# Moving the sample's attention from the attention units to the output projection in a one-core streaming encoder layer

## The chip, the cores and the metric

The kernel runs on one core of one Trainium2 chip. The metric is the device time of one execution in microseconds (us); the number given for a kernel is the median of its runs.

## What is computed

One layer of an encoder over two groups of tokens that share their weights: a prompt of 1,024 tokens and a sample of 64 tokens with a cache of 1,024 past tokens. The model width is 1,024, the feed-forward width 4,096, everything in float32. Shift, scale and gate come from a small product with `w_ada`.

```
h   = RMSNorm(x) * (1 + scale1) + shift1
u   = h @ w_in                -> diff q|k|v (4 heads of 128), sb q|k|v (8 heads of 64)
diff: p = softmax(q k^T / 8 - slope * dist, chunk mask), a = p0 - lam * p1, o = RMSNorm(a v) * 0.8
sb:   w[i,j] = sigmoid(z[i,j]) * product over later keys of sigmoid(-z), o = w v
x   = x + gate1 * RMSNorm(mix @ w_out)
x   = x + gate2 * RMSNorm(relu(h2 @ w_up)^2 @ w_down)
outputs: x of prompt and sample, and the new k and v of both groups
```

The prompt attends to itself. The sample attends to the cache and to itself, so each of its heads has 1,088 keys.

## The kernel before

Every product is done in split form: a float32 matrix is cast into a high part (ACT, L64) and a low part, the difference (DVE or POOL, L65), and two or three matmuls of these parts are summed in PSUM. The 1,088 tokens lie in nine tiles of 128, the ninth holding the sample's 64.

Attention is cut into eight units u of 128 columns: units 0 to 3 are one differential head each (class Diff), units 4 to 7 two stick-breaking heads each (class Stick). A unit's section is eight steps. A step has two parts: `score` (products of queries and keys, then softmax or sigmoids and a scan) and `apply` (transposes of the weights on PE, their split, product with the values). One loop runs through all steps and merges the apply of step j with the score of step j+1; beside them a filler hands out pieces of the projections of the next unit, so that PE has work while DVE and ACT prepare weights. Scans (L712) and the products after them (L713) are on DVE, sigmoids (L738, L739) and exponentials (L624) on ACT.

The sample is one more kind of step, class Sample, one per unit, put into the sections: sample u lies in the section of unit u+1, sample 3 at the end of its own section, sample 7 before the last step. Its score transposes the cache's keys (L813), splits them, and multiplies (L836 to L838); for units 4 to 7 it takes sigmoids (L867, L868), masks the corner on POOL (L720), and scans; its apply transposes (L586), multiplies with the values (L602, L603) and reduces; `finish` writes the result `ms` to `mixD` in DRAM (L908). Its split keys and values take four of the ten large buffers "qk" that also hold the units' Q and K.

After the last step comes the output projection. The weights w_out are split (POOL for the low part), `mixD` is read back and split for three groups of tiles, and for each of nine tiles PE does 48 matmuls (32 for the ninth) into two PSUM banks "pv" and "qk":

```
for m in range(NTT):
    ...
    ps = bank(f"py{m}{i}", "qk" if i else "pv")
    ...
    if pend:
        tail_T(*pend.pop())
```

After a tile's matmuls follows its epilogue: product with the gate (DVE, L1076), squares and sums (ACT, L87), an inverse root on POOL (L80, L81), the addition to x (DVE, L1079), squares again, again POOL, a scaling (ACT, L1083). One tile later `tail_T` transposes the result and makes h2 from it (L163, L276, L278, L64, L65). Then come sixteen blocks of the feed-forward part, up (L303 to L305) and down (L1145 to L1148).

The order of the instructions on each engine is fixed when the kernel is built: a scheduler takes the instructions by their place in the program and by its own estimate of when each can start, and an engine then works through its queue in the order that results. A buffer tag with n buffers lets the next tile of that tag begin when the oldest is released.

Of the kernel before, what the change touches and what calls it, by code (L numbers as in the profile page):

```python
# [10 lines left out]
F32 = mybir.dt.float32  # L11
# [23 lines left out]
def build(tc, I, O):  # L35
# [755 lines left out]
    class Sample:  # L791
# [6 lines left out]
        def cache(self):  # L798
            u = self.u
            fam, uc = family(u)  # L800
            kr = big(f"ckr{u}", "raw", [P, 8, P], F32)
            load(kr, ck[fam][:, :, uc : uc + P])
            vr = big(f"cvr{u}", "raw", [P, 8, P], F32)
            load(vr, cvv[fam][:, :, uc : uc + P])
            kn = small([P, 2, TS], f"kn{u}", "kf")
            load(kn, smD[u])
            vn = small([TS, P], f"vn{u}", "kf")
            load(vn, smV[u])
            kh, kl = (big(f"ck{x}{u}", "qk", [P, PAST]) for x in "hl")
            for half in range(2):  # L810
                ps = bank(f"pck{u}{half}", "qk")
                for i in range(4):
                    nc.tensor.transpose(ps[:, i * P : (i + 1) * P], kr[:, 4 * half + i, :], ident)  # L813
                cols = slice(512 * half, 512 * half + 512)
                split(ps, kh[:, cols], kl[:, cols])
# [6 lines left out]
            self.keys = [(kh[:, 0:512], kl[:, 0:512]), (kh[:, 512:], kl[:, 512:]), (Kn[:, 0, :], Kn[:, 1, :])]  # L822
            Vn = brief([TS, 2, P], f"Vn{u}", "Vn", F32R, bufs=1)
            split(vn, Vn[:, 0, :], Vn[:, 1, :])
            V = []
            for i in range(2):
                v = big(f"cv{u}{i}", "qk", [P, 4, 2, P])
                split(vr[:, 4 * i : 4 * i + 4], v[:, :, 0, :], v[:, :, 1, :], el=nc.gpsimd)
                V.append(v)
            self.V = lambda j: V[j // 4][:, j % 4] if j < 8 else Vn  # L830
# [45 lines left out]
        def apply(self):  # L876
            u, s = self.u, self.s
            po = bank(f"po{self.name}", "pv")
# [85 lines left out]
    for u in range(7):  # L964
        if u != 3:
            sections[u + 1].insert((1,1,2,2,1,1,2)[u], Sample(u))
    sections[3].append(Sample(3))
    sections[7].insert(8, Sample(7))
    steps = [st for sec in sections for st in sec]
    need = []  # L970
    for u in range(8):
        sec = [st for st in sections[u] if not isinstance(st, Sample)]
        for st, g in zip((sec[0], sec[2], sec[6]), range(3)):
            need.append((steps.index(st), (u, g)))
# [53 lines left out]
    for g, (c0, n) in enumerate(GRP):  # L1028
        hi, lo = mT[g]
        for k in range(KT):  # L1030
            st = big(f"mst{g}{k}", "s", [P, 512], F32)
            load(st[:, :n], mixD[k, :, c0 : c0 + n])
            split(st[:, :n], hi[:, k, :n], lo[:, k, :n])
            if g == 2:
                nc.vector.tensor_tensor(hi[:, k, 320:384], st[:, 256:320], fr(hi[:, k, 256:320]), ALU.subtract)
# [11 lines left out]
    for m in range(NTT):  # L1047
# [6 lines left out]
        for i in range(2):  # L1054
            ps = bank(f"py{m}{i}", "qk" if i else "pv")
            cols = slice(512 * i, 512 * i + 512)
            for k in range(KT):
# [14 lines left out]

# [11 lines left out]
        pend.append((m, xn))  # L1084

# [184 lines left out]
```

## Time and profile before

| | |
|---|---|
| median of 3 runs | 1585.93 us (1582.46 to 1588.23) |
| the profiled execution, its own time | 1589.58 us |
| its span in the profile | 1587.9 us |
| PE busy | 1517.0 us, 96% of the span |
| DVE busy | 987.2 us, 62% |
| ACT busy | 703.3 us, 44% |
| POOL busy | 366.7 us, 23% |

The profile is of one execution. PE is the matmul engine, DVE the vector engine, ACT the scalar engine, POOL the general engine, SP the one that issues DMAs. Busy time counts a matmul from its start to its modelled end, and matmuls overlap, so that 96% does not mean that PE has no room. PEclk is the granted clock of PE as a share of 2.4 GHz; its lower level is 1.2 GHz, and a value between is a mean over the stretch. The windows view gives for a stretch its length, then the busy time (and the number of instructions) of PE, of PEld (weight loads, which overlap PE), DVE, ACT and POOL, then PEclk, the share of DMA time and GB/s. In the timeline a row is start, length, engine, line, operation, out<-in and shape, with the idle time before it and who ended it in brackets. A line such as L712 is a line of the kernel before.

### The profile page before, as it was taken

To read this page: it belongs to the slowest core of one execution; us is meant where nothing else is said; L and a number is where in the kernel's file an instruction comes from. 1 tells how busy PE (TensorE), PEld (TensorE's weight loads), DVE (VectorE), ACT (ScalarE), POOL (GpSimd) and SP (SyncE) were. 2 spreads that over 40 slices of the span, in tenths; PEclk is the share of its full clock that TensorE was granted. 3 is DMA by queue.
4 is the path that set the end of the run, shared out by engine and by line. 5 is a ranking of instruction groups with operands and counts; after the bars stand their busy time and mean duration, and the time that the engine had idled before them with its cause. 6 is when DMAs were issued, how large, how long until landed. Compare 5 with 4: busy or idle time off the path is not lost.

```text
span 1587.9 us, 23684 instructions
## 1 busy us (share of the span) xinstructions
PE 1517.0 (96%) x8682; PEld 1357.9 (86%) x8682; DVE 987.2 (62%) x1880; ACT 703.3 (44%) x1665; POOL 366.7 (23%) x580
## 2 busy tenths in 40 slices
PE   6899999999999999789999999999999999999998
PEld 3689988988888889667889888999999899999896
DVE  3777676778789888995552455445544445544447
ACT  3867675766666667656563221121221121221132
POOL 0444352526353434451120000000000000000003
PEclk9999999998999999879999999999999999999999
DMA  9322142432322222364220222021111011111025
GB/s 309 115 60 87 55 116 84 135 95 76 95 74 85 69 70 78 103 208 161 97 63 27 80 80 78 17 79 53 54 42 52 28 41 53 54 41 53 27 80 179
DMA packets 152518, 133.22 MB, mean 84 GB/s; under 512 B 11233, under 2 KB 136274, under 8 KB 152402
## 3 DMA queue, kind: packets, MB, share of 16 engines
q1 hardware_dynamic: 152402, 131.71, 27.2%
q8 instruction: 68, 1.11, 0.3%
q14 instruction: 48, 0.39, 0.1%
HBM read 108.59 MB, written 23.09 MB: 83 GB/s over the span
## 4 chain that ended last, share of the span: by engine, by line
PE 74%; DVE 12%; issue 4%; ACT 3%; DMA 2%; POOL 1%; SPq 0%; POOLq 0%; DVEq 0%; ACTq 0%
PE pu L303 8%; PE pu L304 8%; PE pu L305 8%; PE pd L1145 8%; PE pd L1146 8%; PE pd L1148 7%; DVE k L712 4%; PE py L1059 2%; PE py L1060 2%; PE pt L586 2%; DVE s L713 2%; PE py L1062 2%; PE pq L304 1%; PE pq L303 1%; PE pq L305 1%
## 5 line engine op out<-in xcount | busy, mean ns | idle before, releaser
L1152 DVE TENSOR_TENSOR acc<-pd,acc 128x512 f32<-128x512 f32 x252 | 171.9, 687 | 113.3 <-PE pd L1148 107.2
L1130 ACT ACTIVATE sq<-pu 128x384 f32<-128x384 f32 (+1 forms) x96 | 45.2, 471 | 310.8 <-PE pu L305 310.8
L1131 DVE TENSOR_TENSOR sq<-sq 128x384 f32<-128x384 f32 (+1 forms) x96 | 72.1, 751 | 174.7 <-ACT sq L1130 174.7
L65 DVE TENSOR_TENSOR al<-pt,ah 128x512 fp32r<-128x512 f32 (+2 forms) x128 | 75.5, 599 | 25.7 <-ACT ah L64 24.9
L575 PE MATMUL pz<-K,Q 128*128 128x512 f32 (+2 forms) x192 | 74.8, 393 | 6.4 <-ACT k L739 2.2
L64 ACT CAST ah<-pt 128x512 fp32r<-128x512 f32 (+2 forms) x128 | 65.4, 523 | 33.6 <-PE pt L586 23.2
L586 PE MATMUL pt<-ident,s 128*128 128x128 f32 x432 | 73.7, 288 | 3.3 <-DVE s L713 2.6
L624 ACT ACTIVATE s<-s,mn 128x512 f32<-128x512 f32 (+3 forms) x96 | 58.5, 611 | 26.7 <-DVE mn L660 25.4
L576 PE MATMUL pz<-Kl,qz 128*128 128x512 f32 (+2 forms) x192 | 69.8, 369 | 0.0
L712 DVE TENSOR_TENSOR_SCAN k<-k 128x127 f32<-128x127 f32 (+3 forms) x64 | 62.1, 980 | 4.3 <-POOL k L720 4.0
L713 DVE TENSOR_TENSOR s<-s,k 128x383 f32<-128x383 f32 (+3 forms) x96 | 62.9, 662 | 1.4
L586 PEld LDWEIGHTS pt<-ident,s 128*128 128x128 f32 x432 | 53.1, 147 | 7.6 <-DVE s L713 3.3
L65 DVE TENSOR_TENSOR rl<-sq,rh 128x384 fp32r<-128x384 f32 x64 | 35.7, 558 | 37.9 <-ACT rh L64 37.9
L738 ACT ACTIVATE s<-pz 128x512 f32<-128x512 f32 (+2 forms) x96 | 48.1, 501 | 16.5 <-PE pz L576 12.0
L575 PEld LDWEIGHTS pz<-K,Q 128*128 128x128 f32 x192 | 38.3, 200 | 15.1 <-ACT k L739 4.5
L64 ACT CAST rh<-sq 128x384 fp32r<-128x384 f32 x64 | 32.9, 514 | 40.2 <-DVE sq L1131 38.2
L739 ACT ACTIVATE k<-pz 128x512 f32<-128x512 f32 (+2 forms) x96 | 48.4, 504 | 4.9 <-DVE k L712 4.0
L442 POOL CAST qz<-Q 64x256 fp32r<-64x256 f32 x64 | 34.7, 542 | 66.3 <-PE pz L576 63.9
L760 PE MATMUL po<-al,V 128*128 128x256 f32 (+1 forms) x160 | 43.5, 306 | 6.7 <-DVE al L65 6.6
L759 PE MATMUL po<-ah,V 128*128 128x256 f32 (+1 forms) x160 | 44.9, 292 | 0.5 <-ACT ah L64 0.5
L720 POOL TENSOR_SCALAR_AFFINE_SELECT s<-s 128x128 f32<-128x128 f32 x64 | 30.1, 470 | 63.6 <-ACT s L738 62.9
L660 DVE CUSTOM_DVE_ANT_0 s<-pz,T 128x512 f32<-128x512 f32 (+3 forms) x64 | 37.2, 585 | 10.8 <-PE pz L576 10.3
(1227 smaller groups left out, 5211.3 us busy)
## 6 DMA issues: line engine op xcount, KB each, us to landing
arr<-in_w_ada SPq DMA_DIRECT2D x16, 512.0 KB
arm<-in_w_ada SPq DMA_DIRECT2D x16, 512.0 KB
ar<-in_w_ada SPq DMA_DIRECT2D x10, 512.0 KB
mixD<-mx SPq DMA_DIRECT2D x32, 128.0 KB
xr<-in_x_prompt SPq DMA_DIRECT2D x16, 256.0 KB
xD<-xr SPq DMA_DIRECT2D x16, 256.0 KB
xy<-xD SPq DMA_DIRECT2D x8, 512.0 KB
out_y_prompt<-xy SPq DMA_DIRECT2D x16, 256.0 KB
```

The source lines that it names most:

```text
L64: (eh or nc.scalar.copy)(hi, src)
L65: (el or nc.vector).tensor_tensor(lo, src, fr(hi), ALU.subtract)
L303: mm(ps[:, :n], lhsT=wh[:, k, :], rhs=hh[:, k, :n], start=(k == 0), stop=False)
L304: mm(ps[:, :n], lhsT=wh[:, k, :], rhs=hl[:, k, :n], start=False, stop=False)
L305: mm(ps[:, :n], lhsT=wl[:, k, :], rhs=hh[:, k, :n], start=False, stop=(k == 7))
L575: mm(ps[:, :w], lhsT=S["Q"][m][:, qt], rhs=S["Kd"][m][:, c0 : c0 + w], start=True, stop=False)
L586: nc.tensor.transpose(pt[:kr, i * P : (i + 1) * P], a, ident)
L712: nc.vector.tensor_tensor_scan(k, k, k, 1.0 if c == n - 1 else kp[c + 1][:, 0:1], ALU.mult, ALU.bypass)
L1145: mm(ps, lhsT=rh[:, off : off + P], rhs=wh[:, cols], start=(j == 0), stop=False)
L1146: mm(ps, lhsT=rh[:, off : off + P], rhs=wl[:, cols], start=False, stop=(m == 8 and end))
L1148: mm(ps, lhsT=rl[:, off : off + P], rhs=wh[:, cols], start=False, stop=end)
L1152: nc.vector.tensor_tensor(acc[m][:, cols], ps, acc[m][:, cols], ALU.add)
```

## The change

The eight samples leave the sections. After the weights w_out and the prompt's part of `mixD` have been read, a new loop runs the samples' applies and scores, merged as the steps were, and the output projection's token tiles 0 to 7 become generators that the same filler hands out between them, each counted as 10.9 us, the samples as 6.3 us. The sample's columns of `mixD` are read and split after sample 7, and only then comes tile 8. The sample's split keys become four tiles of 512 columns with the tag "s" (11 buffers, shared with the sample's weights and tables, with x, xn and the pieces of `mixD`); its values become one tile with the tag "v" (2 buffers, of which the gate's rows hold one), split at the start of apply and not in score. A token tile's two PSUM banks come from "pj" (2 banks in all) and no longer from "pv" and "qk", of which the samples now use these.

```diff
-            kh, kl = (big(f"ck{x}{u}", "qk", [P, PAST]) for x in "hl")
+            self.keys = []
             for half in range(2):
...
+                kh, kl = (big(f"ck{x}{u}{half}", "s", [P, 512]) for x in "hl")
+                split(ps, kh, kl)
+                self.keys.append((kh, kl))
...
+        def values(self):
...
+            V = big(f"cv{u}", "v", [P, 8, 2, P])
             for i in range(2):
-                v = big(f"cv{u}{i}", "qk", [P, 4, 2, P])
-                split(vr[:, 4 * i : 4 * i + 4], v[:, :, 0, :], v[:, :, 1, :], el=nc.gpsimd)
+                js = slice(4 * i, 4 * i + 4)
+                split(self.vr[:, js], V[:, js, 0, :], V[:, js, 1, :], el=nc.gpsimd)
...
         def apply(self):
             u, s = self.u, self.s
+            self.values()
...
-    for u in range(7):
-        if u != 3:
-            sections[u + 1].insert((1,1,2,2,1,1,2)[u], Sample(u))
-    sections[3].append(Sample(3))
-    sections[7].insert(8, Sample(7))
...
-    for m in range(NTT):
+    def out_tile(m):
...
-            ps = bank(f"py{m}{i}", "qk" if i else "pv")
+            ps = bank(f"py{m}{i}", "pj")
...
+                yield 0.68
...
+    for m in range(8):
+        fill.add(out_tile(m), 10.9)
+    samples = [Sample(u) for u in range(8)]
+    drain(samples[0].score())
+    for j, st in enumerate(samples):
+        nxt = samples[j + 1] if j < 7 else None
+        ratio = fill.left() / sum(x.cost for x in samples[j:])
+        for c in merge(st.apply(), nxt.score() if nxt is not None else ()):
+            fill.spend(c * ratio)
+        if j:
+            samples[j - 1].finish()
+    samples[7].finish()
+    for x in fill.todo:
+        drain(x[0])
+    fill.todo = []
+    mixed(2, TP, TS, 256, "s")
+    drain(out_tile(8))
```

The first place where the order changes is PE at the end of attention. Names: `po_31` is the product of the last stick-breaking step, `py` a token tile of the output projection, `pck`, `pzS`, `ptS` the sample's transposed keys, its scores and its transposed weights. Before:

```order
L759 MATMUL po_31_9135<-ah_313_9181,V_7846 128x256
L760 MATMUL po_31_9135<-al_313_9182,V_7846 128x256
L759 MATMUL po_31_9135<-ah_313_9181,V_7846 128x128
L760 MATMUL po_31_9135<-al_313_9182,V_7846 128x128
L1059 MATMUL py_9455<-wo0h,mh_9258 128x512
L1060 MATMUL py_9455<-wo0l,mh_9258 128x512
L1062 MATMUL py_9455<-wo0h,ml_9259 128x512
```

With the change:

```order
L759 MATMUL po_31_8069<-ah_313_8115,V_7055 128x128
L760 MATMUL po_31_8069<-al_313_8116,V_7055 128x128
L840 MATMUL pzS_8334<-ckh_8304,bd 128x512
L841 MATMUL pzS_8334<-ckl_8305,bd 128x512
L842 MATMUL pzS_8334<-ckh_8304,bd 128x512
L840 MATMUL pzS_8339<-ckh_8313,bd 128x512
L841 MATMUL pzS_8339<-ckl_8314,bd 128x512
L842 MATMUL pzS_8339<-ckh_8313,bd 128x512
L840 MATMUL pzS_8344<-Kn_8317,bd 128x64
L841 MATMUL pzS_8344<-Kn_8317,bd 128x64
L842 MATMUL pzS_8344<-Kn_8317,bd 128x64
L813 MATMUL pck_8383<-ident,ckr_8375 128x128 x4
```

Before, token tiles follow the last step at once. Now the scores of sample 0 and the keys of sample 1 stand there, and no `py` comes until two products of sample 2 are through, 53 rows after the last of `po_31`.

The second place is ACT in the epilogue of a token tile; `jk` are the squares, `xn` the scaling that ends the epilogue, `xtb` belongs to `tail_T`. Before:

```order
L87 ACTIVATE jk_9638,sso_9641<-py_9586 128x512
L87 ACTIVATE jk_9637,ssb_9652<-xr_0_9557 128x512
L87 ACTIVATE jk_9638,ssb_9652<-xr_1_9558 128x512
L278 ACTIVATE xtb_9616<-ptb_9611,Bm_500,Am_499 128x128
L278 ACTIVATE xtb_9628<-ptb_9623,Bm_500,Am_499 128x128
L1083 ACTIVATE xn_0_9635<-xr_0_9557,rsb_9656 128x512
L1083 ACTIVATE xn_1_9636<-xr_1_9558,rsb_9656 128x512
```

With the change, beside samples 4 and 5 (`ss`, `sk`, `skt` are the sigmoids of the three pieces of sample 5, the last of them the corner of 64 keys):

```order
L871 ACTIVATE ss_1_9622<-pzS_9648 128x512
L872 ACTIVATE sk_1_9625<-pzS_9648 128x512
L64 CAST bd<-kn_9744 64x64 x2
L871 ACTIVATE sst_9623<-pzS_9669 128x64
L64 CAST Kn_9853<-kn_9744 128x64
L87 ACTIVATE jk_9544,ssb_9559<-xr_0_9328 128x512
L87 ACTIVATE jk_9545,ssb_9559<-xr_1_9329 128x512
L64 CAST ahS_9587<-ptS_9582 128x512
L1089 ACTIVATE xn_0_9542<-xr_0_9328,rsb_9563 128x512
L1089 ACTIVATE xn_1_9543<-xr_1_9329,rsb_9563 128x512
L64 CAST ahS_9644<-ptS_9642 64x128
L872 ACTIVATE skt_9626<-pzS_9669 128x64
```

The sigmoids of the next sample now stand between the parts of one epilogue, and the corner's sigmoid `skt` behind the scaling `xn`.

The third place is DVE in the sample's scan, which starts at the corner `skt` and goes to `sk_1` and `sk_0`. Before, in an attention section (`al` and `mx` are of prompt steps):

```order
L712 SCALAR_TENSOR_TENSOR skt_7151<-skt_7151 128x64
L713 TENSOR_TENSOR sst_7148<-sst_7148,skt_7151 128x63
L712 SCALAR_TENSOR_TENSOR sk_1_7150<-sk_1_7150,skt_7151 128x512
L713 TENSOR_TENSOR ss_1_7147<-ss_1_7147,sk_1_7150 128x511
L712 SCALAR_TENSOR_TENSOR sk_0_7149<-sk_0_7149,sk_1_7150 128x511
L779 TENSOR_TENSOR mx_30_6949<-po_31_6954,ot_31_7064 64x256
L65 TENSOR_TENSOR al_000_7074<-pt_000_7069,ah_000_7073 128x384
L713 TENSOR_TENSOR ss_0_7146<-ss_0_7146,sk_0_7149 128x511
```

With the change, for sample 5:

```order
L712 SCALAR_TENSOR_TENSOR skt_9626<-skt_9626 128x64
L65 TENSOR_TENSOR h2l_9517<-xtb_9523,h2h_9516 128x4x128
L713 TENSOR_TENSOR sst_9623<-sst_9623,skt_9626 128x63
L712 SCALAR_TENSOR_TENSOR sk_1_9625<-sk_1_9625,skt_9626 128x512
L65 TENSOR_TENSOR h2l_9517<-xtb_9535,h2h_9516 128x4x128
L65 TENSOR_TENSOR alS_9588<-ptS_9582,ahS_9587 128x512
L65 TENSOR_TENSOR ckl_9754<-pck_9748,ckh_9753 128x512
L1082 TENSOR_TENSOR xn_0_9781<-py_9572,Gg_8288 128x512
L713 TENSOR_TENSOR ss_1_9622<-ss_1_9622,sk_1_9625 128x511
L712 SCALAR_TENSOR_TENSOR sk_0_9624<-sk_0_9624,sk_1_9625 128x511
L65 TENSOR_TENSOR alS_9645<-ptS_9642,ahS_9644 64x128
L713 TENSOR_TENSOR ss_0_9621<-ss_0_9621,sk_0_9624 128x511
```

The same six instructions of the scan now have the halves of h2, a low part of the weights (`alS`), of the next sample's keys (`ckl`) and the gate's product of a token tile between them.

## Rows read from the trace of the kernel before

**Rows 1.** Windows view: the two halves of attention, and the output projection.
```profile
100.00:390.00 290.00, 278.99 (x1824) 257.39 (x1823) 206.64 (x578) 194.46 (x568) 122.56 (x197) 0.97 0.33 95
...
390.00:719.00 329.00, 301.36 (x1906) 273.52 (x1906) 292.69 (x472) 208.60 (x484) 139.44 (x220) 0.92 0.33 99
...
740.00:807.00 67.00, 67.00 (x316) 55.06 (x315) 33.39 (x61) 39.94 (x98) 11.35 (x36) 1.00 0.25 83
```

**Rows 2.** Timeline of PE: last attention matmul, first matmul of the feed-forward part.
```profile
718.99 0.27 PE L760 MATMUL po<-al,V 128*128 128x128 f32 x1
...
807.47 0.34 PE L303 MATMUL pu<-h2h,wu00h 128*128 128x384 f32 x1
```

**Rows 3.** Timeline of PE: start and length of close-packed matmuls and transposes.
```profile
658.93 0.28 PE L759 MATMUL po<-ah,V 128*128 128x256 f32 x1
...
659.05 0.28 PE L760 MATMUL po<-al,V 128*128 128x256 f32 x1
...
659.62 0.39 PE L575 MATMUL pz<-K,Q 128*128 128x512 f32 x1
...
659.85 0.39 PE L576 MATMUL pz<-Kl,qz 128*128 128x512 f32 x1
...
661.25 0.60 PE L586 MATMUL pt<-ident,s 128*128 128x128 f32 x4
...
661.69 0.60 PE L813 MATMUL pck<-ident,ckr 128*128 128x128 f32 x4
```

**Rows 4.** Tile view and groups by line: the sample's operations (min/median/max or mean ns).
```profile
L868 ACT ACTIVATE sk<-pzS x8: 592/593/636, 450.2 to 672.2; 128x512 f32<-128x512 f32 x8
...
L713 DVE TENSOR_TENSOR ss<-ss,sk x8: 660/673/814, 458.9 to 683.7; 128x511 f32<-128x511 f32 x8
...
L712 DVE TENSOR_TENSOR_SCAN sk<-sk,skt x4: 1271/1278/1312, 457.4 to 676.5; 128x512 f32<-128x512 f32 x4
...
L712 DVE TENSOR_TENSOR_SCAN sk<-sk,sk x4: 1268/1290/3409, 459.5 to 679.5; 128x511 f32<-128x511 f32 x4
...
L720 POOL TENSOR_SCALAR_AFFINE_SELECT skt<-skt x8: 232/235/237, 456.4 to 673.8; 64x64 f32<-64x64 f32 x8
...
L712 DVE TENSOR_TENSOR_SCAN skt<-skt x4: 292/292/294, 456.9 to 674.1; 128x64 f32<-128x64 f32 x4
...
L65 DVE TENSOR_TENSOR alS<-ptS,ahS 128x512 fp32r<-128x512 f32 x16 | 10.7, 681 | 1.1 <-ACT ahS L64 1.1
...
L64 ACT CAST ahS<-ptS 128x512 fp32r<-128x512 f32 x16 | 9.0, 598 | 1.4 <-PE ptS L586 1.3
```

**Rows 5.** Timeline: the epilogue of one token tile (start, us).
```profile
800.14 0.60 ACT L87 ACTIVATE jk<-py 128x512 f32<-128x512 f32 x1 [4.37 <-DVE xn L1076]
...
800.73 1.74 ACT L278 ACTIVATE xtb<-ptb,Bm,Am 128x128 f32<-128x128 f32 x4
...
802.04 1.41 DVE L1079 SCALAR_TENSOR_TENSOR xr<-xn,rso,xr 128x512 f32<-128x512 f32 x2
...
805.73 1.34 ACT L1083 ACTIVATE xn<-xr,rsb 128x512 f32<-128x512 f32 x2
```

**Rows 6.** Timeline and tile view: POOL beside DVE, and the sample's value splits.
```profile
458.94 2.89 POOL L65 TENSOR_TENSOR wq6l<-wq6r,wq6h 128x1024 fp32r<-128x1024 f32 x1
...
459.50 3.41 DVE L712 TENSOR_TENSOR_SCAN sk<-sk,sk 128x511 f32<-128x511 f32 x1
...
L65 POOL TENSOR_TENSOR cv<-cvr,cv x16: 1276/1291/2192, 137.5 to 666.3; 128x512 fp32r<-128x512 f32 x16
```

**Rows 7.** Chain that ended last: a write to DRAM and the load behind it.
```profile
655.71 1.89 DMA smV<-ov
...
657.62 1.94 DMA vn<-smV
```

**Rows 8.** Windows view: the end of the last attention section.
```profile
660.00:680.00 20.00, 15.12 (x92) 11.41 (x90) 18.45 (x29) 13.85 (x28) 11.12 (x16) 0.82 0.56 184
...
680.00:694.00 14.00, 9.29 (x43) 8.14 (x42) 13.97 (x15) 8.62 (x15) 10.47 (x8) 0.62 0.41 125
```

More of the change, by code (lines that the diff above doesn't have):

```diff
@@ L813, in cache @@
                     nc.tensor.transpose(ps[:, i * P : (i + 1) * P], kr[:, 4 * half + i, :], ident)
-                cols = slice(512 * half, 512 * half + 512)
-                split(ps, kh[:, cols], kl[:, cols])
+                kh, kl = (big(f"ck{x}{u}{half}", "s", [P, 512]) for x in "hl")
+                split(ps, kh, kl)
+                self.keys.append((kh, kl))
                 yield 0.43
@@ L821, in cache @@
                 split(kn[r, 0, :], bd[r, 0, r], bd[r, 1, r])
-            self.keys = [(kh[:, 0:512], kl[:, 0:512]), (kh[:, 512:], kl[:, 512:]), (Kn[:, 0, :], Kn[:, 1, :])]
+            self.keys.append((Kn[:, 0, :], Kn[:, 1, :]))
+            self.vr, self.vn = vr, vn
+        def values(self):
+            u = self.u
             Vn = brief([TS, 2, P], f"Vn{u}", "Vn", F32R, bufs=1)
-            split(vn, Vn[:, 0, :], Vn[:, 1, :])
-            V = []
+            split(self.vn, Vn[:, 0, :], Vn[:, 1, :])
+            V = big(f"cv{u}", "v", [P, 8, 2, P])
             for i in range(2):
-                v = big(f"cv{u}{i}", "qk", [P, 4, 2, P])
-                split(vr[:, 4 * i : 4 * i + 4], v[:, :, 0, :], v[:, :, 1, :], el=nc.gpsimd)
-                V.append(v)
-            self.V = lambda j: V[j // 4][:, j % 4] if j < 8 else Vn
+                js = slice(4 * i, 4 * i + 4)
+                split(self.vr[:, js], V[:, js, 0, :], V[:, js, 1, :], el=nc.gpsimd)
+            self.V = lambda j: V[:, j] if j < 8 else Vn
         def products(self, c):
@@ L971, in build @@
     for u in range(8):
-        sec = [st for st in sections[u] if not isinstance(st, Sample)]
+        sec = sections[u]
         for st, g in zip((sec[0], sec[2], sec[6]), range(3)):
@@ L1027, in build, with mixed @@
     mT = group_tiles("m")
-    for g, (c0, n) in enumerate(GRP):
+    def mixed(g, c0, n, o, name):
         hi, lo = mT[g]
         for k in range(KT):
-            st = big(f"mst{g}{k}", "s", [P, 512], F32)
+            st = big(f"mst{name}{k}", "s", [P, 512], F32)
             load(st[:, :n], mixD[k, :, c0 : c0 + n])
-            split(st[:, :n], hi[:, k, :n], lo[:, k, :n])
-            if g == 2:
-                nc.vector.tensor_tensor(hi[:, k, 320:384], st[:, 256:320], fr(hi[:, k, 256:320]), ALU.subtract)
+            split(st[:, :n], hi[:, k, o : o + n], lo[:, k, o : o + n])
+            if c0 == TP:
+                nc.vector.tensor_tensor(hi[:, k, 320:384], st[:, :n], fr(hi[:, k, o : o + n]), ALU.subtract)
+    for g, (c0, n) in enumerate(GRP):
+        mixed(g, c0, min(n, TP - c0), 0, f"{g}")
     GG1 = gate("g1", 0, "v")
```

## The prediction

> **What bounds the kernel now.** I read the windows view first, cut at the borders of the stages. In the first half of attention (units 0 to 3) PE is busy for 279 of 290 us and DVE for 207; in the second (units 4 to 7) DVE is busy for 293 of 329 us, 89%, and PE for 301 at a mean granted clock of 0.92; in the output projection PE is busy for all of 67 us at full clock, while DVE has 33 us and ACT 40 us of work [rows 1]. So the first half is PE's, the second is DVE's with PE close behind, and the projection is PE's alone. The timeline of PE gives the two borders that the sum uses: the last attention matmul starts at 719.0 us and the first of the feed-forward part at 807.5 us, 88.5 us later [rows 2]. Behind that border nothing is changed except tile 8's h2, which is needed last in the first block.
>
> The idea that the rows support is plain: move 36 us of DVE work out of a stage where DVE is full into one where it has room. The question is whether PE stays fed there.
>
> **What a sample costs.** On PE, close-packed starts are 0.23 us apart for 512 columns, 0.12 for 256, and 0.44 for four transposes [rows 3]. A sample has 16 transposes of full blocks and one small (1.9), six products of 512 columns (1.4) and three of 64 (0.3 at 0.12 each), and nine pairs in the apply (2.1): 5.7 us, 45 for eight. On DVE a stick-breaking sample has three scans (0.29, 1.28, 1.29), two products of 0.67 and a small one of about 0.2, four low parts at 0.68 (the keys' taken like the weights') and some seven small operations at about 0.25 [rows 4]: 9 us.
>
> **Attention without samples.** First half: PE's 5.7 us of four samples, 23 us, and by the idle 11 us there [rows 1] at most 34. Second half: DVE's 4 x 9 = 36 us at 89% busy, 40 us; at least PE's 23 us, if DVE's room only becomes idle, at most 48, if the clock of 0.92 rises too. I take 23 + 40 = 63, between 46 and 82. The projection's first tile stays beside the last steps, as before. The last attention matmul then comes at 719 - 63 = 656 us. What covered the samples in attention, the filler's projections, is still there for the prompt's steps, so I cost their new order at nothing; if they bunch up, the lower bound of 46 holds it.
>
> **The new stage, on PE alone.** Seven token tiles of 48 matmuls and one of 32, at 0.23 us, are 85 us; samples 45; the tail's 72 transposes 8: 138 us. That is the floor, and with it the stage would end at 794 us, 13 us earlier than now. All the rest depends on waits.
>
> **The start.** The order shows the scores of samples 0 and 1 and the apply of sample 0 with no token tile between them. That is one chain: transposes 0.4, two casts and low parts 2.6, products and sigmoids or table sums about 3, exponentials or scans about 4, then again transposes and a split 1.7 (rates of [rows 3, 4]). I put it at 13 us until tile 1 starts, between 8 (PE work alone) and 20.
>
> **The period.** Then one token tile runs with the apply of one sample and the score of the next, from one sample's first transposes to the next one's, six times. PE's work in it is 10.9 + 5.7 = 16.6 us, and this is the lower bound. I follow the order on ACT and DVE for samples 4 and 5:
> (a) transposes 0.4, the cast 0.6, a product of the next sample 0.7, two sigmoids 1.2 [rows 3, 4] and three of the tail's pieces of 0.44 [rows 5], 1.3: 4.2 us until ACT reaches the last squares of the token tile.
> (b) the epilogue: from those squares at 800.14 to the end of the scaling at 807.07 it took 6.9 us on an ACT with room [rows 5]; here DVE and ACT come to it late by two more pieces of the tail, so 7.9.
> (c) only then, in ACT's queue, the corner's sigmoid behind a small cast, 0.5, and POOL's two masks, 0.5 [rows 4].
> (d) the scan and its products on DVE, 4.4, and between them the halves of h2, two low parts and a gate's product, five at about 0.7: 7.9.
> Together 21, and an epilogue, a scan and a split wait for each other in one ring, so no filler can shorten it. For the samples that use exponentials the ring has no scan but the three exponentials stand behind the same scaling; I take the same. I take 22 us, between 16.6 and 27 (a token tile's 5 us of matmuls inside the ring in place of beside it): six periods are 132.
>
> One wait is missing in that: the value splits on POOL, now at the start of apply, when DVE scans. A scan that lasts 1.29 as a rule lasted 3.41 beside a POOL difference of 2.89 [rows 4, 6], so the two splits of 1.29 [rows 6] can cost up to 2.6 us in a period, or nothing. I take 1, the last part of the 22 (nearer to the median of 1.29 than to the one long scan), and both ends are inside the bounds. The Trainium skill, "SBUF — State Buffer", section "Who interferes with whom", calls the ports that VectorE and GpSimd share an exclusive lock, held for a whole instruction. By that rule each split that meets an operation with two SBUF inputs would block it to its end, and the sum would be some 10 us later; the rows show one such wait, but also samples' scans that passed unharmed (median 1.29), so I do not take it in full.
>
> **The end.** The apply of sample 7 with tile 7: 10.9 + 2.1 + 1 of PE and the last split, 16 us. Then a serial stretch that was hidden before: two copies of the result (0.8 together; each is shorter than the cast of 0.6 in [rows 4]), its write to DRAM and the load behind it (1.9 each [rows 7]), the cast and two differences, some 5.5 us in which PE has nothing in its queue but tile 8, and tile 8 itself, 32 x 0.23 = 7.4: 13 us. SP is passed in the same order, with the eight small loads queued behind the write.
>
> **The sum.** 656 + 13 + 132 + 16 + 13 = 830 us against 807.5: 22.5 us later. The profiled execution took 1589.6 us, 3.7 above the median of 1585.9 us; set against the median the forecast is **1608 us**, slower by 1.4%. So the 63 us are won in attention, and the stage behind it grows from 88.5 to 174 us.
>
> **Rivals.**
> *PE stays fed, faster.* DVE and ACT get through the ring in the shadow of the token tiles, with periods of 17 us and attention shorter by 70: 649 + 13 + 102 + 16 + 13 = 793, 14.5 earlier, 1571 us. For it: DVE and ACT have half of the projection's time free [rows 1]. Against it: the order, in which the corner's sigmoid waits for the epilogue. The point of balance is a period of 18.3 us with my other terms: (807.5 - 656 - 42) / 6.
> *PE falls to its lower clock.* At the end of attention PE is busy for 15.1 of 20 us at 0.82 and then for 9.3 of 14 us at a granted clock of 0.62, between its levels of 1.2 and 2.4 GHz [rows 8]. The new stage has 16.6 of 22 us. At 0.75 PE's work in a period is 22 us, and the part of it inside the ring grows: a period of 28, 36 us more, 1644 us. The Trainium skill, "TensorE: Matmul & The Clock Gate", section "Loop structure matters more than you think", says that a loop that waits before its matmuls runs cold; [rows 8] agree with it for the stretch before 694 us.
> *No change.* Gains and waits cancel, periods near 18 us: 1586 us.
> That the change does not do what it says I rule out: the order has no sample in the sections.
>
> **How the numbers follow.** Forecast (slower, without a great loss of clock): 0.57. Lower clock: 0.12. Faster: 0.21. No change: 0.10. A measurement of this kernel tells about 0.3%, 4.8 us, from no change. So faster 0.21, same 0.10, slower 0.69. The range: from 1574, inside the faster case, to 1638, which has periods of 27 us (30 us above the forecast) and most of the lower clock; a tenth lies outside at each end. The forecast's own range is 1592 to 1638.
>
> **What would show it.** Right: no wait for samples between 100 us and the end of attention, which comes at 656 (646 to 673) us; DVE's share in the second half not above 90%; then some 170 us until the first matmul of the feed-forward part, with PE busy for four fifths of it or less, and repeating waits of `poS` and `ptS` for DVE and ACT; an idle stretch of PE of about 5 us before tile 8. Wrong: a stage under 150 us with PE busy throughout (then the ring is not one, and the first rival holds), or an end of attention after 680 us (then DVE was not what held the second half).

## The result, and the profile after

The changed kernel takes 1625.8 us (median of 4 runs, 1624.1 to 1629.3) against 1585.9 us: ratio 1.0256 with an interval of 1.0230 to 1.0283, slower by 40 us. The forecast was 1608 us, slower, in a range of 1574 to 1638. The profiled execution took 1629.3 us, 3.5 above its median; its span is 1627.5 us.

The windows view of the changed kernel, cut at 390 us as in [rows 1] and at its own end of attention (columns as there):

```profile
100.00:390.00 290.00, 276.98 (x1810) 255.25 (x1811) 200.10 (x526) 180.27 (x515) 113.90 (x196) 0.98 0.28 82
390.00:651.00 261.00, 238.59 (x1553) 217.52 (x1551) 236.19 (x374) 171.27 (x382) 103.21 (x172) 0.95 0.31 93
651.00:847.00 196.00, 161.58 (x787) 128.34 (x787) 117.03 (x254) 117.14 (x306) 54.56 (x101) 0.91 0.38 117
```

In the second window DVE is busy for 236 of 261 us, still 90%. The 390 us are no border of a stage: the first sigmoids of unit 4 start at 369.0 us before and at 334.8 with the change. So the two windows do not tell the two halves of attention apart. Over both, DVE is busy for 436 us in place of 499, 63 us less, and attention is 68 us shorter.

The stage behind attention is 196 us long; PE is busy for 162 of them, 82%, at a mean granted clock of 0.91, where the projection of before had PE busy throughout at full clock.

The timeline of PE gives the borders. The first row answers to the first of [rows 2], the last to the second; between them stand the first transposes of weights of samples 1 and 7, which bound the six periods:

```profile
650.80 0.28 PE L760 MATMUL po<-al,V 128*128 128x128 f32 x1
...
677.13 0.66 PE L586 MATMUL ptS<-ident,ss 128*128 128x128 f32 x4 [0.19 <-ACT ss L624]
...
814.12 1.12 PE L586 MATMUL ptS<-ident,ss 128*128 128x128 f32 x4 [5.58 <-DVE ss L713]
...
846.27 0.69 PE L303 MATMUL pu<-h2h,wu00h 128*128 128x384 f32 x1 [0.83 <-DVE ysm L1077]
```

The last attention matmul comes 68.2 us earlier than before (719.0 to 650.8), the first of the feed-forward part 38.8 us later (807.5 to 846.3). What follows is equal: 781.2 us of span against 780.4. So 68 us were won and 107 us lost. The forecast had 63 and 85.5.

The border also cuts the projection at another place. The windows view of its products `py` alone, up to the end of attention, before and with the change:

```profile
600.00:719.10 119.10, 19.01 (x72) 13.53 (x72) 0.00 (x0) 0.00 (x0) 0.87 0.45 139
600.00:650.90 50.90, 14.31 (x48) 8.88 (x48) 0.00 (x0) 0.00 (x0) 0.87 0.64 205
```

A tile and a half (72 products) used to run beside the last steps of attention, now it is one tile (48). The 24 products behind the border are 5.5 us of PE's work at 0.23 us.

The 107 us can be split by PE. In the stage before, from 719.0 to 807.5 us, PE was busy for 86.4 of 88.5 us. Now it is busy for 161.1 of 195.5. So 32 us are idle time. Of the other 75 us, 51 are work: 45.6 of eight samples by the prediction's count, and the 5.5. The last 24 us are products that start further apart than in [rows 3], a part of them at the lower clock.

| stretch of the sum | forecast | measured |
|---|---|---|
| end of attention | 656 | 650.8 |
| start, to the first `ptS` of sample 1 | 13 | 26.3 |
| six periods | 132 | 137.0 |
| last apply, tiles 7 and 8 | 29 | 32.2 |
| first `pu` | 830 | 846.3 |

The six periods are 19.2, 23.2, 21.4, 20.6, 27.5 and 25.1 us. What PE waited for in this stage is told by the waits view (total us, times, longest):

```profile
PE pzS L840 <- DVE ckl L65: 8.0, 4, 5.8
PE ptS L586 <- DVE ss L713: 6.8, 3, 5.6
PE poS L603 <- DVE alS L65: 4.4, 2, 3.4
```

These are the three largest of PE's waits, and each is a wait of a sample's small step for DVE. A token tile's own products waited 0.6 us in all, for the squares of the tile before.

**The start** is the stretch that was sized wrong. The timeline of all engines, in order of time:

```profile
653.07 2.67 POOL L65 TENSOR_TENSOR cv<-cvr,cv 128x512 fp32r<-128x512 f32 x2 [8.31 <-ACT cv L64]
...
653.85 2.17 DVE L65 TENSOR_TENSOR ml<-mst,mh 128x256 fp32r<-128x256 f32 x2 [0.82 <-ACT mh L64]
...
656.05 1.29 DVE L65 TENSOR_TENSOR ckl<-pck,ckh 128x512 fp32r<-128x512 f32 x2
...
656.88 0.77 PE L840 MATMUL pzS<-ckh,bd 128*128 128x512 f32 x1 [5.81 <-DVE ckl L65]
...
657.45 0.63 PE L841 MATMUL pzS<-ckl,bd 128*128 128x512 f32 x1
...
657.87 0.63 PE L842 MATMUL pzS<-ckh,bd 128*128 128x512 f32 x1
...
660.32 0.41 ACT L64 CAST mh<-mst 128x256 fp32r<-128x256 f32 x1 [5.17 <-DMA mst<-mixD]
660.75 0.42 DVE L65 TENSOR_TENSOR ml<-mst,mh 128x256 fp32r<-128x256 f32 x1 [3.42 <-ACT mh L64]
661.12 0.69 DVE L858 CUSTOM_DVE_ANT_0 ss<-pzS,Ts 128x512 f32<-128x512 f32 x1
...
661.87 0.42 PE L840 MATMUL pzS<-Kn,bd 128*128 128x64 f32 x1 [2.09 <-DVE smn L858]
...
665.87 1.97 PE L586 MATMUL ptS<-ident,ss 128*128 128x128 f32 x8 [1.07 <-ACT ss L624]
...
671.92 0.67 DVE L858 CUSTOM_DVE_ANT_0 ss<-pzS,Ts 128x512 f32<-128x512 f32 x1
...
676.26 0.72 ACT L624 ACTIVATE ss<-ss,smn 128x512 f32<-128x512 f32 x1 [0.76 <-DVE smn L858]
```

PE waits 5.8 us for the low part `ckl` of sample 0's keys. That stands on DVE behind the prompt's pieces `ml`, two of which take 2.17 us beside the POOL split of the values. Then ACT's `mh` waits 5.2 us for the last piece of `mixD` to come from DRAM; `ml` waits for `mh`, and behind `ml` in DVE's queue stands the first table sum of sample 0 (661.12), for which PE waits again (661.87). Sample 0's first transposes come at 665.9, 15.1 us after the last attention matmul. Then sample 1 goes through the same steps behind sample 0's: its first table sum comes at 671.9, its first exponentials at 676.3 and its first transposes at 677.1, another 11.3 us later.

After the first wait products of 512 columns start 0.43 us apart, not 0.23 as in [rows 3]. The windows view has PE at its lower clock level of 1.2 GHz, 0.50 of the upper, from 657 to 668 us:

```profile
657.00:661.00 4.00, 2.79 (x6) 1.69 (x6) 0.58 (x2) 0.41 (x1) 0.00 (x0) 0.50 0.89 294
662.00:668.00 6.00, 4.77 (x20) 3.66 (x20) 2.78 (x13) 4.94 (x13) 0.00 (x0) 0.50 0.40 110
```

**A period** of the long kind, from sample 5's first transposes (761.51) to those of sample 6 (789.05):

```profile
761.51 0.60 PE L586 MATMUL ptS<-ident,ss 128*128 128x128 f32 x4
...
765.85 0.50 PE L1065 MATMUL py<-wo0h,mh 128*128 128x512 f32 x1 [0.42 <-ACT jk L87]
...
770.59 0.60 PE L163 MATMUL ptb<-ident,xn 128*128 128x128 f32 x4
...
771.23 0.60 ACT L872 ACTIVATE sk<-pzS 128x512 f32<-128x512 f32 x1 [3.27 <-PE ptb L163]
...
772.38 0.41 DVE L276 TENSOR_SCALAR xtb<-ptb,Am,Bm 128x128 f32<-128x128 f32 x1 [4.92 <-PE poS L603]
...
778.76 1.34 ACT L1089 ACTIVATE xn<-xr,rsb 128x512 f32<-128x512 f32 x2 [0.82 <-POOL rsb L81]
...
780.15 0.22 ACT L872 ACTIVATE skt<-pzS 128x64 f32<-128x64 f32 x1
...
781.01 0.29 DVE L712 TENSOR_TENSOR_SCAN skt<-skt 128x64 f32<-128x64 f32 x1 [4.52 <-POOL skt L720]
...
784.45 0.33 PE L603 MATMUL poS<-cv,alS 128*128 128x128 f32 x1 [3.37 <-DVE alS L65]
```

From 765.85 to 770.59 PE works through 20 products of a token tile. Behind them in its queue stand the transposes `ptb` of the finished tile and the products `poS`; ACT waits 3.27 us for the one, DVE 4.92 us for the other. Then the epilogue runs to its scaling `xn` (778.76), behind which the corner's sigmoid `skt` stands, 18.6 us after the period's start. The scan begins at 781.0, 19.5 us after it, and PE, whose tile is through by now, waits 3.4 us for a low part that stands between the scans.

**The end** was read wrongly in its mechanism. The round trip through DRAM is there:

```profile
834.08 0.30 PE L910 MATMUL pmS<-ident,sod 128*64 128x128 f32 x1 [2.01 <-DVE sod L900]
...
834.91 0.37 SPq L913 DMA_DIRECT2D mixD<-ms  x1
...
840.27 0.24 ACT L64 CAST mh<-msts 128x64 fp32r<-128x64 f32 x1
...
842.27 0.39 PE L1066 MATMUL py<-wo7l,mh 128*128 128x512 f32 x1
```

From the issue of the write (834.91) to the cast of what came back (840.27) are 5.4 us, but PE did not idle: tile 8 takes the eight k in turn, only the last belongs to sample 7, and its last product starts at 842.3.

### The profile page after: what moved, and what is told of

Read it like the earlier page. It is cut to its first block, busy times and chain, and to the rows that moved or that the text cites. A ratio compares the mean times of both kernels' runs of the same rounds, so it can differ in the third digit from the quotient of the medians.

```text
span 1627.5 us, 23753 instructions
## 1 busy us (share of the span) xinstructions
PE 1527.8 (94%) x8682; PEld 1358.0 (83%) x8682; DVE 989.7 (61%) x1888; ACT 710.4 (44%) x1675; POOL 355.1 (22%) x580
## 3 DMA queue, kind: packets, MB, share of 16 engines
q1 hardware_dynamic: 153554, 131.71, 26.3%
## 4 chain that ended last, share of the span: by engine, by line
PE 52%; DVE 3%; issue 2%; ACT 1%; POOL 1%; DMA 0%; DVEq 0%; POOLq 0%; ACTq 0%
PE pu L303 8%; PE pu L304 8%; PE pu L305 8%; PE pd L1170 7%; PE pd L1171 7%; PE pd L1173 6%; PE py L1065 2%; PE py L1066 2%; PE py L1068 1%; DVE sk L712 1%; PE ptS L586 1%; PE poS L602 1%; DVE ss L713 0%; DMA wd01r<-in_w_down 0%; PE ptb L163 0%
## 5 line engine op out<-in xcount | busy, mean ns | idle before, releaser
L713 DVE TENSOR_TENSOR s<-s,k 128x127 f32<-128x127 f32 (+3 forms) x96 | 71.8, 752 | 1.7
L712 DVE TENSOR_TENSOR_SCAN k<-k 128x127 f32<-128x127 f32 (+3 forms) x64 | 52.6, 823 | 12.1 <-POOL k L720 11.4
L64 ACT CAST rh<-sq 128x384 fp32r<-128x384 f32 x64 | 32.9, 515 | 40.7 <-DVE sq L1156 38.8
L660 DVE CUSTOM_DVE_ANT_0 s<-pz,T 128x512 f32<-128x512 f32 (+3 forms) x64 | 37.4, 586 | 12.6 <-PE pz L576 12.1
```

The lines of the kernel that those rows point to most:

```text
L64: (eh or nc.scalar.copy)(hi, src)
```

## Experiments

The theory after the result: a sample's chain (transposes, split, products, sigmoids, scan) and a token tile's epilogue make one ring on DVE and ACT, and that sets the period. Rivals: the two banks "pj", the POOL splits, PE's clock, and a start that any token tile could fill. Each kernel was timed against the kernel before.

### Does the interleaving hide anything?

`samples_alone`: the filler hands out no token tile beside the samples.

```diff
         for c in merge(st.apply(), nxt.score() if nxt is not None else ()):
-            fill.spend(c * ratio)
+            pass
```

> The eight samples run one behind the other with no token tile between them, and the nine token tiles follow. Theory (one ring of sample and token tile): the period of 22.8 us holds about 10 us of a token tile's epilogue, so samples alone have a period of 12 to 13 us between the first ptS of one and of the next. Stage: start 26 + seven periods of 12.5, 88, + last apply 8 + eight tiles of 10.9 and one of 7.4, 95 = 217 us against 195.5 in the changed kernel: 1647 us. Rival (PE's own work and the two banks pj set the period, not the ring): a sample has 5.7 us of PE work and 9 us of DVE work, so samples alone come every 9 us and the stage is 26 + 63 + 8 + 95 = 192 us: 1622 us.

Measured: 1639.2 us, ratio 1.0323 (1.0292 to 1.0354). The timeline of PE shows the first transposes of samples 4 and 7, three periods apart, and behind them one token tile after another:

```profile
716.98 1.97 PE L586 MATMUL ptS<-ident,ss 128*128 128x128 f32 x8 [0.21 <-DVE ss L713]
...
753.99 1.97 PE L586 MATMUL ptS<-ident,ss 128*128 128x128 f32 x8 [5.48 <-DVE ss L713]
...
774.10 1.03 PE L163 MATMUL ptb<-ident,xn 128*128 128x128 f32 x8
...
786.08 1.03 PE L163 MATMUL ptb<-ident,xn 128*128 128x128 f32 x8
```

Samples 1 to 7 start 10.0, 11.2, 17.2, 12.0, 12.6 and 12.4 us apart, 12.6 in the mean, as the theory had it and not the rival's 9; a token tile with its tail takes 12.0 (774.10 to 786.08). One behind the other they are 24.6 us. The changed kernel, which interleaves them, needs 22.8. **The interleaving hides 1.8 us of 12.6 in a period**, though PE has only 5.7 us of work in a sample. The stage is 207 us here (653.0 to 860.0), against 217 in the theory's sum and 195.5 in the changed kernel.

### The two PSUM banks

`banks_back`:

```diff
-            ps = bank(f"py{m}{i}", "pj")
+            ps = bank(f"py{m}{i}", "qk" if i else "pv")
```

> A token tile's two banks come from pv and qk again, as in the kernel before; in the built order a tile of 22 products then stands ahead of sample 0's last products. Rival (the two banks pj hold up the token tiles): periods fall to 19 us or less, 20 us in all, 1606 us or less. Theory (the ring sets the period, whatever bank the tile has): the periods stay at 22 to 23.5 us, and only the start gains the 10 us of the tile that now lies in it, or loses them again where pv and qk are short: 1611 to 1626 us.

Measured: 1646.1 us, ratio 1.0376 (1.0345 to 1.0407), 20 us slower than the changed kernel, which neither had foreseen. Its periods are 17 to 29 us, 24.5 in the mean. In one of them:

```profile
718.18 0.51 ACT L64 CAST bd<-kn 64x64 fp32r<-64x64 f32 x2 [4.24 <-PE pzS L841]
718.29 0.28 DVE L858 CUSTOM_DVE_ANT_0 sst<-pzS,Tst,smn 128x64 f32<-128x64 f32 x1 [6.23 <-PE pzS L842]
```

ACT waits 4.2 us and DVE 6.2 us for the corner's products, which stand in PE's queue behind a run of token-tile products that lasts from 711.2 to 717.7; then, at 723.0, PE waits 3.5 us for DVE. So the periods do not fall, and the 0.6 us that token-tile products wait in the changed kernel leave the banks "pj" little to hold up. The waits view of `banks_back` shows a price of shared banks:

```profile
PE py L1065 <- DVE smn L858: 4.0, 2, 2.3
PE poS L602 <- ACT jk L87: 3.0, 4, 0.9
```

Token-tile products wait for a sample's table sum, and a sample's products for a token tile's squares, 7 us together, now that both use the same banks. How the rest of the 20 us divides between the banks and the other order that the scheduler makes with them is not separated.

### The start

`score0_first`: sample 0's score is written ahead of the third group of `mixD`.

```diff
-    for g, (c0, n) in enumerate(GRP):
+    for g, (c0, n) in enumerate(GRP[:2]):
...
     drain(samples[0].score())
+    mixed(2, GRP[2][0], TP - GRP[2][0], 0, "2")
```

> The score of sample 0 is put ahead of the reading of the third group of mixD, so that its splits no longer stand behind casts that wait for the last pieces of mixD. Theory (the start of 26.3 us is long because ACT's and DVE's queues hold casts that wait for those DMAs): start 14 to 18 us, 1615 us. Rival (the start is the chain of two scores and one apply itself): start 24 us or more, 1622 to 1628 us.

Measured: 1622.5 us, ratio 1.0221 (1.0192 to 1.0250). The last attention matmul to sample 0's first `ptS` falls from 15.1 to 7.3 us, but from there to sample 1's it grows from 11.3 to 14.7: the pieces of the third group now stand there. The start is 22.0 us, in neither range (14 to 18, and 24 or more); the queue heads explain 4 of its 13 surplus us.

`start_fed`: token tiles also beside sample 0's score.

```diff
-    drain(samples[0].score())
+    ratio = fill.left() / sum(x.cost for x in samples)
+    for c in samples[0].score():
+        fill.spend(c * ratio)
```

> All eight samples are moved, and the score of sample 0 also has a token tile beside it, so that one of the later samples has none. Theory (sample and token tile hardly overlap: 12.6 and 12.0 us alone give 22.8 us together): the tile adds 10 us to the start and takes 10 us from a later period: 1621 to 1630 us. Rival (the start of 26.3 us is idle time of PE that any tile can fill): the first ptS of sample 1 comes no later than now, and the whole is 10 to 13 us shorter: 1612 to 1616 us.

Measured: 1608.9 us, ratio 1.0145 (1.0121 to 1.0168), 17 us less than the changed kernel; more than even the rival had, but not by the rival's way. The start is 31.7 us, 5.4 longer, and it holds 26 of a tile's 48 products, 6.0 us at 0.23. They stand in one run from 674.5 us to sample 1's first transposes at 680.6, and the idle time of PE in the start is 10.9 us, where it was 10.7. So the run fills none of it. The gain lies behind: the six periods are 120.7 us (mean 20.1), 16 us less with 9 products more, and the end is 22.9, 9 us less with 35 products fewer. Windows of the stage, and the timeline of the period from sample 5 to 6:

```profile
649.00:824.00 175.00, 154.27 (x786) 125.56 (x785) 116.24 (x252) 114.69 (x303) 58.02 (x101) 0.92 0.42 133
```
```profile
761.51 0.60 PE L586 MATMUL ptS<-ident,ss 128*128 128x128 f32 x4
...
771.95 0.22 ACT L872 ACTIVATE skt<-pzS 128x64 f32<-128x64 f32 x1
...
772.78 0.29 DVE L712 TENSOR_TENSOR_SCAN skt<-skt 128x64 f32<-128x64 f32 x1 [0.42 <-PE poS L602]
...
782.14 0.60 PE L586 MATMUL ptS<-ident,ss 128*128 128x128 f32 x4
```

PE is busy for 154 of 175 us. The corner's sigmoid comes 10.4 us after the period's start, where it was 18.6, and the scan to the next transposes 9.4 (8.0 before): nearly the same operations (45 products of token tiles in place of 48), in another phase, take 20.6 us in place of 27.5. So the ring has no fixed length: what PE's queue holds between its small steps is a part of it.

`fed_corner`: `start_fed` with the corner first.

```diff
-                for c in range(3):
+                for c in (2, 0, 1):
                     ps = self.products(c)
                     nc.scalar.activation(s[c], ps, AF.Sigmoid)
```

> As start_fed, with the corner of 64 keys first in the score of samples 4 to 7, so that its sigmoids no longer stand behind the scaling of a token tile in ACT's queue. Theory (step c of the prediction: the scan waits for the corner, and the corner for the epilogue): 0.5 to 1.5 us less in each of four periods: 1603 to 1607 us. Rival (that wait is covered once the tiles are spread another way): within 2 us of start_fed, 1607 to 1611 us.

Measured: 1606.2 us, ratio 1.0123 (1.0102 to 1.0143), 2.8 us less. The number is the theory's, but the intervals overlap, and the profiles do not show the gain where the theory puts it: the six periods are 122.8 us here and 120.7 in `start_fed`. So no difference between the two can be told. They are the best kernels with all samples moved.

### The scan and the value splits

`no_scan`:

```diff
-                stick(s, kp)
+                nc.vector.tensor_tensor(s[2], s[2], kp[2], ALU.mult)
```

> Leaves out the running product and its products with the sigmoids for samples 4 to 7 (one small product of 64 columns stands for them). Theory as predicted (scan, split and epilogue are one ring on DVE and ACT): every period from sample 3 on, 20.6, 27.5 and 25.1 us and the two beside them, is shorter by 3.5 to 4.4 us: 14 to 18 us in all, 1608 to 1612 us. Theory now (the loss lies in how PE's runs of token-tile products and the small steps stand in one queue): only the idle time of PE that ends with the scan's product goes, 8 to 11 us: 1614 to 1618 us. Rival (PE's clock and work alone set the periods): 0 to 4 us, 1622 us or above.

Measured: 1610.3 us, ratio 1.0157 (1.0126 to 1.0189), 15.5 us less: the sum that the predicted ring gives, though the interval reaches the 1614 us of the second theory. It does not come evenly: the six periods are 19.2, 21.3, 19.7, 20.6, 23.5 and 18.5 us, so 4.0 and 6.6 us come from the two long ones and nothing from the one between samples 4 and 5, the very one that the prediction followed. 2.0 us come from the second, which has no scan. In the long ones the scan is in the ring; in the others another part decides.

`values_dve`:

```diff
-                split(self.vr[:, js], V[:, js, 0, :], V[:, js, 1, :], el=nc.gpsimd)
+                split(self.vr[:, js], V[:, js, 0, :], V[:, js, 1, :])
```

> The changed kernel with the low parts of the sample's values made on DVE and not on POOL, so that no POOL split runs beside a scan. Theory (the splits cost little: in the changed kernel's projection three DVE operations, 1.58, 1.22 and 2.27 us where their like take 0.68, 0.2 and 1.28, are longer by 2.9 us in all, and DVE now has 1.4 us more work for each sample): within 6 us of the changed kernel, 1620 to 1632 us. Rival (every split blocks DVE to its end, as the higher estimate of the prediction had it, 10 us in all): 1612 to 1618 us.

Measured: 1620.6 us, ratio 1.0221 (1.0194 to 1.0248), 5 us less than the changed kernel, with overlapping intervals; no product of the scan is longer than 0.69 us any more. The changed kernel's timeline beside a POOL split, against [rows 4] and [rows 6]:

```profile
808.79 2.93 POOL L65 TENSOR_TENSOR cv<-cvr,cv 128x512 fp32r<-128x512 f32 x2
809.07 1.53 DVE L713 TENSOR_TENSOR ss<-ss,sk 128x511 f32<-128x511 f32 x1
...
810.53 2.27 DVE L712 TENSOR_TENSOR_SCAN sk<-sk,sk 128x511 f32<-128x511 f32 x1
```

The product (0.67 as a rule) takes 1.53, the scan (1.28) takes 2.27. Both start while a split runs. The count in the expectation was short. In the whole stage there are also `ml` at 653.85 (2.17 for 0.8, two of them), `bd` at 674.75 (1.27 for 0.23), `so` at 698.08 (1.40 for 0.28) and 741.18 (0.85), `ss` at 739.17 (1.58) and 787.49 (1.51), and `sod` at 761.13 (2.37 for 0.42, two of them) and 789.52 (0.92): 10 us in all, beside seven of the eight pairs of splits. An operation that was under way when a split began kept its length (the scan at 737.86, 1.27), and so did one that reads PSUM (`ckl` at 697.47, 0.69). At most half of the 10 us is seen in the time: without the splits on POOL, DVE has 1.4 us more work for each sample, and not every operation of DVE is waited for.

### How many samples to move

`sticks_out` moves samples 4 to 7 alone, `two_out` 6 and 7, `one_out` 7; the others stay in the sections as before. In `two_out` and `one_out` the first score has token tiles too, as in `start_fed`. In `one_late` sample 7 starts behind 16 us of token tiles, and its column is split ahead of the last of them.

```diff
+    OUT = (7,)
...
-    samples = [Sample(u) for u in range(8)]
-    drain(samples[0].score())
+    samples = [Sample(u) for u in OUT]
+    fill.spend(16)
+    ratio = 0.6 * fill.left() / sum(x.cost for x in samples)
+    for c in samples[0].score():
+        fill.spend(c * ratio)
...
+    samples[-1].finish()
+    mixed(2, TP, TS, 256, "s")
     for x in fill.todo:
         drain(x[0])
```

> Only samples 4 to 7 are moved; samples 0 to 3 stay in the sections with their tiles of before. Theory: the second half of attention gains its 45 us, the first half nothing, so the last attention matmul comes at about 674 us. With two token tiles to a sample PE has 27.5 us of work in a period and the ring of 22.8 us fits beside it: 674 + start 26 + three periods of 27.5, 83, + last apply and a tile 16 + end 10 = 809 us until the first pu, against 807.5 before and 846 changed: 1588 us. Rival (lower clock of PE or the start set the stage, not the number of rings): periods of 33 us and more, 1605 us or above. Rival (each half of attention gains in proportion): last attention matmul at 685 us or later, 1599 us.

Measured: 1614.2 us, ratio 1.0172 (1.0145 to 1.0199). Attention ends at 683.7, the stage is 148.4 us, and the two full periods are 32.9 and 35.0 us: with two token tiles to a sample a period is still 3 to 5 us longer than PE's work (two times 12.0 and 5.7). The theory's 1588 fails. The rival's value is met, though its cause is not settled: the granted clock is 0.93 from 700 to 800 us. The end of attention, 35 us earlier, lies between the theory's 674 and the second rival's 685, next to the latter.

> Only sample 7 is moved, and its score too has token tiles beside it. Theory now (a moved sample costs PE's 5.7 us, and beyond that what its own chain of 12.6 us and one token tile of 12 us fail to overlap; with all token tiles beside one sample its small instructions never hold PE up): attention ends 9 to 12 us earlier, the stage behind it grows by 6 to 8 us: 1580 to 1587 us. Rival (every moved sample loses about 5 us beyond PE's work, and the stage its start of 10 us or more, wherever its tiles are): 1592 us or above.

Measured: 1592.3 us, ratio 1.0041 (1.0027 to 1.0054): again the rival's value. The last attention matmul comes at 695.8, 23 us earlier, and nothing of it reaches the end: the first `pu` comes at 808.7. The windows view before that border, of `py` alone and of all, and the timeline behind it:

```profile
600.00:695.80 95.80, 12.33 (x38) 7.91 (x38) 0.00 (x0) 0.00 (x0) 0.89 0.43 135
...
660.00:680.00 20.00, 11.29 (x61) 8.68 (x61) 19.70 (x21) 10.51 (x19) 12.73 (x10) 0.74 0.44 151
```
```profile
703.50 0.50 PE L851 MATMUL pzS<-ckh,bd 128*128 128x512 f32 x1 [3.23 <-DVE ckl L65]
```

From 660 to 680 us DVE is as full as before ([rows 8] have 18.45 of 20, here 19.70), since the next work moves up, and PE has 11.29 us of work where it had 15.12. Up to the border only 38 products of token tiles are through, where it had been 72. So the border comes earlier in part because 7.8 us of PE's work (34 products at 0.23) has passed behind it, together with the sample's 5.7: 13.5 of the 23 us are no gain at all. Behind the border PE waits 3.2 and 1.0 us for the sample, and from 703 to 709 us its granted clock is 0.59.

> Samples 6 and 7 are moved, fed as in one_out. Theory: attention ends 17 to 20 us earlier, the stage grows by 11.4 us of PE's work and 2 to 6 us of waits: 1580 to 1588 us. Rival (a fixed loss of 5 us a sample and a start of 10 us or more): 1595 us or above.

Measured: 1601.4 us, ratio 1.0105 (1.0084 to 1.0126): the rival's value.

> As one_out, but 16 us of token tiles are handed out ahead of sample 7's score, the sample is through with two token tiles left, and its column of mixD is split before those. Theory (one_out loses its gain in the start of the sample, where PE waits 3.2 us and 1.0 us for ckl and sk and then runs at its lower clock, and 1.8 us ahead of tile 8): these go, 6 to 9 us less than one_out: 1583 to 1586 us, level with the kernel before. Rival (what one_out loses lies at the end of attention, where PE has only 11.3 us of work in 20 and DVE stays full, and that is not touched): within 3 us of one_out, 1589 us or above.

Measured: 1589.4 us, ratio 1.0013 (0.9999 to 1.0028), 2.9 us less than `one_out`: no difference from the kernel before that can be told. In its stage PE no longer waits for the sample's keys and sigmoids, and still nothing is won; that is the rival's reading. Here too 38 products stand ahead of the border, so of the 18.7 us by which it comes earlier (700.3) 13.5 are PE's work that now follows it.

`keys_s_only` is the kernel before with the change's first hunk alone, the keys in tiles "s".

```diff
-            kh, kl = (big(f"ck{x}{u}", "qk", [P, PAST]) for x in "hl")
+            self.keys = []
...
+                kh, kl = (big(f"ck{x}{u}{half}", "s", [P, 512]) for x in "hl")
```

> The kernel before, all samples in the sections, but the sample's split keys in tiles with the tag s and not qk. Theory (what attention gains is the samples' own work on DVE and PE): no difference, 1582 to 1590 us. Rival (a part of the gain is the qk buffers that the samples no longer hold): 1576 us or less. Second rival (the tag s is short in the sections, which is a cost of the new tiles wherever the samples run): 1592 us or above.

Measured: 1591.8 us, ratio 1.0040 (1.0023 to 1.0056), between the theory's range and the second rival's 1592, and next to the latter. It frees two of a sample's four "qk" buffers (the values keep theirs) and takes four of tag "s": in sum 0.4% slower. A gain of the buffers that the tag "s" eats up again is not excluded. No kernel of the study beats the one before.

## Why the prediction was right

**Attention** (forecast 63 us, range 46 to 82; measured 68.2): the sum was right, and DVE's share stayed at 90%, as the reason wants it. The parts were 23 us for samples 0 to 3 and 40 for 4 to 7. `sticks_out`, which moves the second four alone, gives 35; that leaves some 33 for the first four if the two add, so one part made up for the other. And not all of the 68 us is a gain: 24 products of the projection, 5.5 us, passed behind the border with the samples. `keys_s_only` shows no gain of the keys' buffers by themselves.

**The start** is the term that failed: 13 us, "between 8 (PE work alone) and 20", measured 26.3, which is 13.3 us of the 16.3 by which the first `pu` missed; the periods and the end add 8.2, and attention gives 5.2 back. The step took the scores of samples 0 and 1 and one apply for "one chain" and counted its parts once. About 10 us of its parts lead to sample 0's first transposes; they came after 15.1 us. That left some 3 us until sample 1's; it took 11.3 more, since sample 1's table sums and exponentials stand behind sample 0's on DVE and ACT. `samples_alone` agrees: there samples 1 to 3, with no token tile beside them, follow each other by 10.0 and 11.2 us. The step also left out what stands in the queues ahead of the chain (the prompt's pieces, among them the one that comes last from DRAM; 4 us by `score0_first`) and that PE runs at its lower clock behind the wait. No run tried the second score apart.

**The period** (forecast 22, measured 22.8 in the mean): the size was right, in part by luck, since the six go from 19.2 to 27.5 us and only the long ones are the ring that was described. Steps (a) to (c) were 13.1 us from the start to the scan, and (d) 7.9 from there to the next transposes. In the long period it was 19.5 and 8.0; the 5 us of token-tile products that I named for the upper bound did stand inside the ring. In `start_fed`, where they did not, it was 11.3 and 9.4. So the sentence that "no filler can shorten it" was wrong. The lower bound of 16.6 was too low as well: it leaves out the tail's eight transposes (0.9), and PE is busy for 19.6 us of a mean period (117.6 of 137.0 us), and for 19.2 in `start_fed`. `no_scan` gives the sum that the ring foresees, but nothing in the period that the prediction worked through.

**The value splits** (1 us in a period, between nothing and 2.6): DVE's operations are longer by 10 us in the stage, some 1.3 in a period; without the splits on POOL the time is 5 us less, with overlapping intervals. By the rule of the Trainium skill, "SBUF — State Buffer", section "Who interferes with whom", that a DVE operation with two SBUF inputs waits to the end of the GpSimd operation, the higher estimate was 10 us. The rows agree with the rule, 2.27 us for a scan of 1.28, and with the 10 us as a sum over DVE's operations; but not all of it is on the way to the end.

**The end** (forecast 29, measured 32.2): the size is near by chance. The 5.5 us idle ahead of tile 8 did not come, since seven eighths of tile 8 do not wait for sample 7. In their place came 2.0 us for `sod` and 3.6 us from the last product's end (842.7) to the first `pu`, which now stands behind the tail of tile 7 in PE's queue and waits for `ysm`.

**The rivals.** *PE stays fed* fell: a mean period of 17 us came in no kernel that runs token tiles beside all samples. The best is 20.1, in `start_fed`, and there PE is fed: it is busy for 115 of the 121 us of the six periods. So 17 was below what PE itself needed there, 19.2. *Lower clock* was partly true: 0.91 in the stage, not the 0.75 that it supposed, and 0.68 in the start (650.8 to 677.1). PE's busy time grew by 24 us beyond its work; how much of that is the clock was not tried.

Beneath all terms lies one sum. Eight samples bring 46 us of PE work into a stage whose PE was full, and 5.5 us of the projection come with them; attention gives 68 back. Of the 17 us between them nothing may be lost, and the changed kernel loses 56: 32 to idle time of PE and 24 to products further apart. `start_fed` loses some 35 (a stage of 175.3 us in place of 88.5, less 51).

## What to carry to other kernels

Work that moves out of a stage where another engine is full gives back that engine's time, but takes its own time on the engine that bounds the new stage, where it had been free; count both before any wait. Two chains that are merged in one in-order queue overlap only if the long run of the one does not stand between the short steps of the other: compare the merged period with the sum of both alone. And a border that comes earlier is not yet time won: count the work that passed behind it, and look at whether the bounding engine is less full in front of it.

## What the runs showed of the hardware

A DVE operation with two SBUF inputs that starts while a POOL split runs is longer by up to 1.1 us (0.67 to 1.53, 1.28 to 2.27, 0.28 to 1.40 and to 0.85); one that was under way already is not (the scan of 1.27 at 737.86).

PE stood idle from 651 to 656.9 us, and behind that its products of 512 columns started 0.43 us apart in place of 0.23, at a granted clock of 0.50. The Trainium skill, "TensorE: Matmul & The Clock Gate", section "Loop structure matters more than you think", has as its bad example a loop with a long wait for a DMA ahead of each matmul, in which PE goes cold. The row agrees, with a wait for DVE in place of one for a DMA.
